# W_out to W_up in a hybrid encoder layer: combinations of normalised tokens moved to GpSimd, and two groups of transposes swapped

## The chip, the core and the metric

The kernel runs on one core of a Trainium2 chip. The metric is device time in microseconds (us) of one execution; lower is better. The core has five engines with instruction queues of their own: TensorE (PE: matrix products, and the transposes of this kernel), VectorE (DVE), ScalarE (ACT), GpSimd (POOL) and SyncE (SP, which here issues DMA transfers). Each queue runs in order, and engines wait for each other by semaphores. TensorE writes to PSUM, of which this kernel has eight banks of 128 x 512 numbers: two each of the kinds mm, s, t and o.

## What is computed

The reference runs one encoder layer over two groups of tokens (a "sample" of 512 and a "prompt" of 1024), with shared weights. This case lies in the prompt, between the output projection and the MLP:

```python
x = x + mixed @ w_out
a = jax.nn.relu(rmsnorm(x, g_mlp) @ w_up)
return x + (a * a) @ w_down
```

`rmsnorm` divides each token by the root of the mean of its squares and multiplies by a gain. The products have float32 accuracy. The kernel reaches it by splitting every operand into a rounded part (hi) and the rest (lo) and adding three products per pair of operands.

## The kernel before

**Place and tiles.** `Halves.project_out` handles the prompt's 1024 tokens in 8 tiles of 128. It takes 16 steps, one for each tile and each half (0 or 1) of the 1024 output channels, in the order that `steps` lists. Step n runs `product(n, t, half)`: 24 matmuls into a bank of kind mm or o (line 128), then VectorE adds the bank to the tile (L1250). The last step is n = 15.

**Normalising.** When a tile has both halves, `norm` (L173 to L183) normalises it: ScalarE squares and sums it (L173), then VectorE takes three one-column steps with one input (L174, L176, L178), six one-column steps with two inputs (L181 and L182, three times each, called the small steps) and one pass over the tile (L183). The eight normalised tiles come in four pairs, i = 0 to 3; k counts the tiles, so a pair is complete at odd k.

**Combinations.** The product with W_up is a fast (Strassen-like) scheme over quarters of the operands. For its seven products it needs quarters of the tokens (b11, b21, b22) and combinations of them (t1, t2, t3, t4). Of each pair the kernel forms four combinations of 128 x 512, tiles h0, h1 or y1, by four subtractions (L1285), all on VectorE:

```python
for to, x, y in ((h1[0], k1, o1), (h2[0], k2, h1[0]), (h2[1], k2, k1), (h1[1], o2, h2[0])):
    nc.vector.tensor_tensor(out=to, in0=x, in1=y, op=ALU.subtract)
```

**Turns.** `turn` transposes one piece of 128 x 512 (L1212): four transposes into a bank of kind t or s, in turn; then two casts on ScalarE (L132) write the hi parts and two subtractions on VectorE (L133, the evictions) the lo parts. The bank is free when all four are done. Which turns follow which product stands in `due`: after step n `flush(n)` runs the list `due[n]`. Pairs 0 and 1 are turned after steps 12 and earlier. After step 15 stand five turns of pair 2 (b22, t1, t2, t3, t4) and behind them two of pair 3 (b11, b21).

**The end of the step.** Then the first group of W_up begins inside `project_out`: the product b11 (12 matmuls into a bank mm), a copy of that bank by ScalarE (L1316, tile r_hi), the product b21 into the same bank, and `flush(16)`, the last five turns, of pair 3. After them `up` goes on with the other products of the scheme; I call that the up phase.

**Weight work beside it.** `ahead` prepares W_up's first group step by step from n = 7 on: ScalarE casts hi parts (L1338), POOL subtracts lo parts and forms weight combinations (L1335; tiles w_raw, x, y). Before the change POOL has nothing else to do here.

**What sets the order.** The program is written as above, and a scheduler of the build then orders each engine's queue by its own estimate of when an instruction can run, within the written dependences; `pinned` and `behind` hold some instructions to a place. So an edit at one place can move instructions of other lines on the same engine.

Of the kernel before, what the change touches and what calls it, by code (L numbers as in the profile page):

```python
# [22 lines left out]
ALU = mybir.AluOpType  # L23
# [1137 lines left out]
class Halves:  # L1161
# [55 lines left out]
    def project_out(self, hp, mp, m, wo):  # L1217

        layer, nc, nt, TH = self.layer, self.nc, self.nt, self.TH
# [8 lines left out]
        due = {}  # L1228

        def flush(n):  # L1230
            with layer.behind(layer.mark((mybir.EngineType.PE,))):
                for x in due.pop(n, ()):
                    self.turn(*x)
# [3 lines left out]
        def product(n, t, half):  # L1237
            ts = slice(t * 128, (t + 1) * 128)
            cs = slice(half * 512, (half + 1) * 512)
            w = wo[4 * half:4 * half + 4]  # L1240
            ops = [(m[kt // 2][0][:, kt % 2, ts], m[kt // 2][1][:, kt % 2, ts], w[kt // 2][0][:, kt % 2], w[kt // 2][1][:, kt % 2])
                   for kt in range(8)]
            if n < 2 and n not in banks:

                banks[n] = layer.psum(("mm", "o")[n % 2])
                layer.mm3(banks[n], ops[:6])
                return
            ps = banks[n] if n < 2 else layer.psum(("mm", "o")[n % 2])
            layer.mm3(ps, ops[6 if n < 2 else 0:], more=n < 2)
            nc.vector.tensor_tensor(out=acc[t][:, cs], in0=acc[t][:, cs], in1=ps, op=ALU.add)  # L1250
# [3 lines left out]
        steps = [(t, 0) for t in order[:nt // 2]]  # L1254
# [8 lines left out]
        for n, (t, half) in enumerate(steps):  # L1263
            product(n, t, half)
            if n == freed:
                b["t2"], b["t3"] = ([layer.pair(hp, [128, 2, TH], "hid", 4) for _ in range(2)] for _ in range(2))
                for x in due.pop("free"):
                    due[n].append(x[:1] + (b[x[1]],) + x[2:])
            flush(n)
            if half:  # L1270
                k = len(hn)
                nc.sync.dma_start(self.sums[t], acc[t])

                hn.append(acc[order[k - 1]] if k else self.tile("y0"))
                layer.norm(acc[t], gain, hn[k])
                i = k // 2
                at = n + (2 if n < len(steps) - 2 else 1)
                k1, k2 = hn[k][:, :512], hn[k][:, 512:]
                if k % 2 == 0:
                    due.setdefault(at, []).extend([(k1, b["b11"], i), (k2, b["b21"], i)])  # L1280
                else:
                    o1, o2 = hn[k - 1][:, :512], hn[k - 1][:, 512:]
                    h1, h2 = ((x[:, :TH], x[:, TH:]) for x in (self.tile("h1"), self.tile("y1" if i == 1 else "h0")))
                    for to, x, y in ((h1[0], k1, o1), (h2[0], k2, h1[0]), (h2[1], k2, k1), (h1[1], o2, h2[0])):
                        nc.vector.tensor_tensor(out=to, in0=x, in1=y, op=ALU.subtract)  # L1285
                    due.setdefault(at, []).append((k2, b["b22"], i))
                    due[at].append((h1[0], b["t1"], i))
                    for src, q in ((h2[0], "t2"), (h2[1], "t3")):
                        if q in b:
                            due[at].append((src, b[q], i))  # L1290
                        else:
                            due.setdefault("free", []).append((src, q, i))
                    due[at].append((h1[1], b["t4"], i))
            if n >= len(steps) // 2 - 1:
                with layer.pinned():
                    next(ahead, None)
# [2 lines left out]
        self.fetch(2)  # L1299
        self.begun = begun = [self.begin(mp)]  # L1300
        self.product(begun[0][0], self.w[0], 0, "b11")
        with layer.pinned():
            next(ahead, None)
        self.second(*begun[0], self.w[0])
# [382 lines left out]
```

## Time and profile before

| | us |
|---|---|
| three timed runs | 2009.88, 2016.78, 2017.57 |
| their median | 2016.78 |
| the profiled execution | 2014.83 |
| its span in the trace | 2013.0 |
| the edited stretch in it (last output product to the up phase) | 1364.5 to 1389.4 |

All times below are counted from the start of the profiled execution's span. Its mean granted TensorE clock is 0.989 of full speed. In a timeline row the first two numbers are start and duration; a row with "x4" stands for four instructions of one kind. In names, `out<-in` gives the tiles written and read. "idle before" is how long the engine stood still, and the name behind the arrow is what released it.

### The profile page before, as it was taken

To read this page: it belongs to the slowest core of one execution; us is meant where nothing else is said; L and a number is where in the kernel's file an instruction comes from. 1 tells how busy PE (TensorE), PEld (TensorE's weight loads), DVE (VectorE), ACT (ScalarE), POOL (GpSimd) and SP (SyncE) were. 2 spreads that over 40 slices of the span, in tenths; PEclk is the share of its full clock that TensorE was granted. 3 is DMA by queue.
4 is the path that set the end of the run, shared out by engine and by line. 5 is a ranking of instruction groups with operands and counts; after the bars stand their busy time and mean duration, and the time that the engine had idled before them with its cause. 6 is when DMAs were issued, how large, how long until landed. Compare 5 with 4: busy or idle time off the path is not lost.

```text
span 2013.0 us, 26474 instructions
## 1 busy us (share of the span) xinstructions
PE 1954.8 (97%) x9635; PEld 1625.1 (81%) x9635; DVE 1098.2 (55%) x1916; ACT 757.7 (38%) x1325; POOL 958.6 (48%) x743
## 2 busy tenths in 40 slices
PE   6999999999999999999999999999999999999997
PEld 4887787888888878888888888887888888888886
DVE  6572445756666552566663225466666666443246
ACT  3564323433332331556552313224333333433342
POOL 3144535467776740223333223413978774644442
PEclk8999999999999999999999999999999999999999
DMA  6666773354444445455555543412444445976663
GB/s 203 170 161 200 217 228 94 96 178 157 147 156 158 150 154 200 114 139 137 135 180 174 136 118 98 160 63 85 177 168 168 172 154 193 299 236 205 194 193 122
DMA packets 275652, 326.50 MB, mean 162 GB/s; under 512 B 42872, under 2 KB 197240, under 8 KB 274968
## 3 DMA queue, kind: packets, MB, share of 16 engines
q1 hardware_dynamic: 261792, 303.92, 47.6%
q0 software_dynamic: 13728, 20.88, 4.5%
q8 instruction: 76, 1.25, 0.3%
q14 instruction: 56, 0.46, 0.1%
HBM read 235.67 MB, written 91.64 MB: 163 GB/s over the span
## 4 chain that ended last, share of the span: by engine, by line
PE 83%; DVE 6%; DMA 4%; issue 2%; ACT 2%; POOL 2%; SPq 0%; POOLq 0%; DVEq 0%; ACTq 0%
PE ps_mm L128 23%; PE ps_o L128 22%; PE ps_s L128 19%; PE ps_t L128 8%; PE ps_mm L487 2%; PE ps_mm L488 2%; PE ps_mm L489 2%; PE ps_o L629 1%; DMA w_raw<-in_w_in 1%; POOL w_lo L152 1%; PE ps_t L609 1%; DMA bm<-g_un 1%; PE ps_t L193 1%; DMA gain<-in_w_fnB 1%; DVE st L182 1%
## 5 line engine op out<-in xcount | busy, mean ns | idle before, releaser
L152 POOL TENSOR_TENSOR w_lo<-w_raw,w_hi 128x1024 fp32r<-128x1024 f32 x84 | 212.7, 2540 | 210.2 <-ACT w_hi L151 180.3
L151 ACT CAST w_hi<-w_raw 128x1024 fp32r<-128x1024 f32 x100 | 104.7, 1048 | 156.4 <-PE ps_s L128 49.9
L487 PE MATMUL ps_mm<-hT,w_hi 128*128 128x512 f32 (+3 forms) x320 | 126.5, 395 | 0.2 <-DVE k L527 0.2
L1088 DVE TENSOR_TENSOR relu<-relu 128x512 f32<-128x512 f32 (+1 forms) x35 | 63.0, 1801 | 108.0 <-ACT relu L1087 108.0
L488 PE MATMUL ps_mm<-hT,w_hi 128*128 128x512 f32 (+3 forms) x320 | 115.2, 360 | 0.0
L489 PE MATMUL ps_mm<-hT,w_lo 128*128 128x512 f32 (+3 forms) x320 | 115.2, 360 | 0.0
L603 ACT ACTIVATE sc<-sc,ast 128x288 f32<-128x288 f32 (+4 forms) x96 | 53.9, 561 | 76.5 <-DVE ast L601 76.2
L1335 POOL TENSOR_TENSOR x<-w_hi,x 128x512 fp32r<-128x512 f32 (+1 forms) x42 | 69.8, 1662 | 23.0 <-ACT x L1338 23.0
L723 POOL MEMSET bm<- 64x96 f32 (+2 forms) x64 | 11.2, 175 | 144.7 <-DVE ast L601 97.7
L152 POOL TENSOR_TENSOR w_lo<-r,w_hi 128x1024 fp32r<-128x1024 f32 x15 | 36.8, 2452 | 87.5 <-ACT w_hi L151 87.5
L629 PEld LDWEIGHTS ps_o<-pt,vb 104*64 104x64 f32 (+6 forms) x576 | 62.3, 164 | 12.2 <-POOL vb L566 4.7
L152 POOL TENSOR_TENSOR w_lo<-w_hi 128x1024 fp32r<-128x1024 f32 x18 | 45.9, 2550 | 50.0 <-ACT w_hi L151 45.8
L152 POOL TENSOR_TENSOR w_lo<-w_lo,w_hi 128x1024 fp32r<-128x1024 f32 x18 | 48.0, 2668 | 45.2 <-ACT w_hi L151 45.2
L489 PEld LDWEIGHTS ps_mm<-hT,w_lo 128*128 128x128 f32 x320 | 60.4, 189 | 8.6
L629 PE MATMUL ps_o<-pt,vb 104*64 104x128 f32 (+6 forms) x576 | 63.4, 245 | 4.0 <-POOL vb L566 2.1
L566 POOL TENSOR_TENSOR vb<-vr,vb 96x384 fp32r<-96x384 f32 (+4 forms) x48 | 48.7, 1032 | 35.6 <-ACT vb L565 30.5
L128 PE MATMUL ps_t<-gate,x 128*128 128x512 f32 x264 | 65.3, 396 | 0.0
L128 PE MATMUL ps_mm<-gate,x 128*128 128x512 f32 x256 | 64.3, 395 | 0.0
L487 PEld LDWEIGHTS ps_mm<-hT,w_hi 128*128 128x128 f32 x320 | 60.9, 190 | 2.2 <-PE ps_s L597 0.4
L488 PEld LDWEIGHTS ps_mm<-hT,w_hi 128*128 128x128 f32 x320 | 61.0, 191 | 1.7
L601 DVE CUSTOM_DVE_ANT_0 sc<-ps_s,bm 128x288 f32<-128x288 f32 (+4 forms) x96 | 46.3, 482 | 24.4 <-PE ps_s L597 13.7
L152 POOL TENSOR_TENSOR w_lo<-raw,w_hi 128x512 fp32r<-128x512 f32 x24 | 35.5, 1485 | 50.5 <-ACT w_hi L151 42.2
(664 smaller groups left out, 5872.4 us busy)
## 6 DMA issues: line engine op xcount, KB each, us to landing
w_raw<-in_w_in SPq DMA_DIRECT2D x56, 512.0 KB
w_raw<-in_w_up SPq DMA_DIRECT2D x34, 512.0 KB
wt<-hn SPq DMA_DIRECT2D x32, 512.0 KB
hidden_prompt<-h SPq DMA_DIRECT2D x32, 512.0 KB
w_hi<-hidden_prompt SPq DMA_DIRECT2D x20, 512.0 KB
w_raw<-hidden_prompt SPq DMA_DIRECT2D x18, 512.0 KB
w_lo<-hidden_prompt SPq DMA_DIRECT2D x18, 512.0 KB
w_raw<-in_w_out SPq DMA_DIRECT2D x16, 512.0 KB
```

Of the source, the lines that this page charges most:

```text
L128: self.nc.tensor.matmul(out, a, b, start=(i == 0 and not more), stop=(i == len(terms) - 1), skip_group_check=more)
L151: nc.scalar.copy(out=hi, in_=raw)
L152: (lo_engine or nc.gpsimd).tensor_tensor(out=lo, in0=raw, in1=hi.bitcast(F32), op=ALU.subtract)
L487: nc.tensor.matmul(ps, a[0], b[0], start=(kt == 0), stop=False)
L488: nc.tensor.matmul(ps, a[0], b[1], start=False, stop=False)
L489: nc.tensor.matmul(ps, a[1], b[0], start=False, stop=(kt == 7))
L566: nc.gpsimd.tensor_tensor(out=lo, in0=vs, in1=hi.bitcast(F32), op=ALU.subtract)
L601: nc.vector.tensor_tensor_reduce(out=sc[:, :W], in0=ps[:, :W], in1=bm[:, :W], scale=1.0, scalar=3e38, op0=ALU.add, op1=ALU.min, accum_out= ...
L603: nc.scalar.activation(out=sc[:, :W], in_=sc[:, :W], func=AF.Exp, bias=st[:, 0:1], scale=-1.0, accum_out=st[:, 1:2])
L629: nc.tensor.matmul(po[:m, j * 128:(j + 1) * 128], v, x, start=(i == 0), stop=(i == len(ops) - 1))
L1088: nc.vector.tensor_tensor(out=r, in0=r, in1=r, op=ALU.mult)
L1335: self.nc.gpsimd.tensor_tensor(out=to, in0=x, in1=y, op=op)
```

## The change

It does two things, both in `project_out`. Of the pairs 0, 1 and 2 all four combinations go from VectorE to POOL, and of pair 3 one (the fourth of the new order) does. And after step 15 the two turns of pair 3 for b11 and b21 come first, then b22 and t1 of pair 2; the other three turns of pair 2 (t2, t3, t4) wait until the product b11 has been issued.

```diff
...
+            if n == len(steps) - 1:
+
+                x = due[n]
+                due[n], due["first"] = x[-2:] + x[:2], x[2:-2]
             flush(n)
...
-                    for to, x, y in ((h1[0], k1, o1), (h2[0], k2, h1[0]), (h2[1], k2, k1), (h1[1], o2, h2[0])):
-                        nc.vector.tensor_tensor(out=to, in0=x, in1=y, op=ALU.subtract)
+
+                    for j, (to, x, y) in enumerate(((h1[0], k1, o1), (h2[0], k2, h1[0]), (h1[1], o2, h2[0]), (h2[1], k2, k1))):
+                        (nc.gpsimd if i < nt // 2 - 1 or j == 3 else nc.vector).tensor_tensor(out=to, in0=x, in1=y, op=ALU.subtract)
...
         self.product(begun[0][0], self.w[0], 0, "b11")
+        flush("first")
```

In the rows of the order below, x_12122 is the second normalised tile of pair 2 and x_12126 the first of pair 3; h_12746 and h_12747 hold pair 2's combinations. On TensorE behind step 15, before the change (ps_mm with gate is b11, then b21):

```order
L1212 MATMUL ps_s<-ident,x_12122 128x128 x4
L1212 MATMUL ps_t<-ident,h_12746 128x128 x4
L1212 MATMUL ps_s<-ident,h_12747 128x128 x4
L1212 MATMUL ps_t<-ident,h_12747 128x128 x4
L1212 MATMUL ps_s<-ident,h_12746 128x128 x4
L1212 MATMUL ps_t<-ident,x_12126 128x128 x4
L1212 MATMUL ps_s<-ident,x_12126 128x128 x4
L128 MATMUL ps_mm<-gate,y_12495 128x512 x8
L128 MATMUL ps_mm<-gate,x_12496 128x512 x4
L128 MATMUL ps_mm<-gate,y_12495 128x512 x8
L128 MATMUL ps_mm<-gate,x_12496 128x512 x4
```

Here all seven turns stand ahead of the first product. On TensorE at the same place, with the change:

```order
L1212 MATMUL ps_s<-ident,x_12126 128x128 x4
L1212 MATMUL ps_t<-ident,x_12126 128x128 x4
L1212 MATMUL ps_s<-ident,x_12122 128x128 x4
L1212 MATMUL ps_t<-ident,h_12746 128x128 x4
L128 MATMUL ps_mm<-gate,y_12495 128x512 x8
L128 MATMUL ps_mm<-gate,x_12496 128x512 x4
L1212 MATMUL ps_s<-ident,h_12747 128x128 x4
L1212 MATMUL ps_t<-ident,h_12747 128x128 x4
L1212 MATMUL ps_s<-ident,h_12746 128x128 x4
L128 MATMUL ps_mm<-gate,y_12495 128x512 x8
L128 MATMUL ps_mm<-gate,x_12496 128x512 x4
```

The two turns of x_12126 have moved from the end of the list to its head, and three turns from before the product to behind its twelve matmuls.

On POOL from pair 1's end to pair 3, before the change, only weight work (L1335) stands there:

```order
L1335 TENSOR_TENSOR x_12562<-w_raw,x_12562 128x512
L1335 TENSOR_TENSOR w_raw<-w_raw 128x512 x2
L1335 TENSOR_TENSOR y_12563<-w_raw,y_12563 128x512
L1335 TENSOR_TENSOR x_12564<-w_raw,x_12564 128x512
L1335 TENSOR_TENSOR x_12565<-w_raw,x_12565 128x512
L1335 TENSOR_TENSOR x_12566<-w_raw,x_12566 128x512
```

The weight combinations (w_raw) follow each other directly. On POOL with the change (L1290 are the combinations, L1341 the weight work; x_12123 is the second normalised tile of pair 3):

```order
L1290 TENSOR_TENSOR h_12746<-x_12122,x_12125 128x512
L1290 TENSOR_TENSOR h_12747<-x_12122 128x512
L1290 TENSOR_TENSOR h_12747<-x_12122,h_12746 128x512
L1341 TENSOR_TENSOR w_raw<-w_raw 128x512
L1290 TENSOR_TENSOR h_12746<-x_12125,h_12747 128x512
L1341 TENSOR_TENSOR w_raw<-w_raw 128x512
L1341 TENSOR_TENSOR y_12563<-w_raw,y_12563 128x512
L1290 TENSOR_TENSOR h_12889<-x_12123 128x512
L1341 TENSOR_TENSOR x_12564<-w_raw,x_12564 128x512
L1341 TENSOR_TENSOR x_12565<-w_raw,x_12565 128x512
L1341 TENSOR_TENSOR x_12566<-w_raw,x_12566 128x512
```

The weight combinations (w_raw) now stand among the token combinations, and the last combination, of pair 3, stands ahead of the lo parts x_12564 to x_12566.

On VectorE around the second tile of pair 3, before the change (x_12123 is written by L183, then come its combinations; ps_s and ps_t are evictions):

```order
L178 TENSOR_SCALAR st<-st 128x1
L181 SCALAR_TENSOR_TENSOR st<-st 128x1
L182 SCALAR_TENSOR_TENSOR st<-st 128x1
L181 SCALAR_TENSOR_TENSOR st<-st 128x1
L182 SCALAR_TENSOR_TENSOR st<-st 128x1
L181 SCALAR_TENSOR_TENSOR st<-st 128x1
L182 SCALAR_TENSOR_TENSOR st<-st 128x1
L183 SCALAR_TENSOR_TENSOR x_12123<-x_12127,st,gain 128x1024
L1285 TENSOR_TENSOR h_12915<-x_12123,x_12126 128x512
L1285 TENSOR_TENSOR h_12916<-x_12123 128x512
L1285 TENSOR_TENSOR h_12916<-x_12123,h_12915 128x512
L1285 TENSOR_TENSOR h_12915<-x_12126,h_12916 128x512
```

Nothing stands between the six small steps. On VectorE with the change (h_12888 and h_12889 are pair 3's combinations):

```order
L133 TENSOR_TENSOR hid_lo<-ps_s,hid_hi 128x2x128
L182 SCALAR_TENSOR_TENSOR st<-st 128x1
L133 TENSOR_TENSOR hid_lo<-ps_t,hid_hi 128x2x128
L181 SCALAR_TENSOR_TENSOR st<-st 128x1
L133 TENSOR_TENSOR hid_lo<-ps_s,hid_hi 128x2x128
L182 SCALAR_TENSOR_TENSOR st<-st 128x1
L133 TENSOR_TENSOR hid_lo<-ps_t,hid_hi 128x2x128
L183 SCALAR_TENSOR_TENSOR x_12123<-x_12127,st,gain 128x1024
L133 TENSOR_TENSOR w_lo<-ps_s,w_hi 128x2x128
L1290 TENSOR_TENSOR h_12888<-x_12123,x_12126 128x512
L1290 TENSOR_TENSOR h_12889<-x_12123,h_12888 128x512
```

The small steps were in one piece and now stand between the evictions of pair 2's last three turns (hid_lo), and one combination has left.

## Rows read from the trace of the kernel before

**Rows 1.** The page, its part 1: busy us (share of the span) xinstructions of each engine.

```profile
PE 1954.8 (97%) x9635; PEld 1625.1 (81%) x9635; DVE 1098.2 (55%) x1916; ACT 757.7 (38%) x1325; POOL 958.6 (48%) x743
```

**Rows 2.** The waits of PE, 1290 to 1420 us: us in total, times, longest us.

```profile
PE ps_s L1212 <- DVE gate L133: 3.6, 1, 3.6
PE ps_mm L128 <- ACT r_hi L1316: 0.7, 1, 0.7
PE ps_t L1212 <- DVE gate L133: 0.6, 1, 0.6
```

**Rows 3.** The timeline of PE: start us, us, engine, line, operation, xcount [idle before <-releaser].

```profile
1350.24 0.60 PE L1212 MATMUL ps_t<-ident,h 128*128 128x128 f32 x4
...
1370.10 0.60 PE L1212 MATMUL ps_s<-ident,x 128*128 128x128 f32 x4
...
1371.40 0.60 PE L1212 MATMUL ps_t<-ident,h 128*128 128x128 f32 x4
1375.61 1.09 PE L1212 MATMUL ps_s<-ident,h 128*128 128x128 f32 x4 [3.60 <-DVE gate L133]
...
1378.05 3.57 PE L128 MATMUL ps_mm<-gate,y 128*128 128x512 f32 x8
...
1383.23 2.12 PE L128 MATMUL ps_mm<-gate,y 128*128 128x512 f32 x8 [0.68 <-ACT r_hi L1316]
...
1386.13 0.60 PE L1212 MATMUL ps_t<-ident,x 128*128 128x128 f32 x4
...
1389.36 0.43 PE L128 MATMUL ps_s<-hid_hi,y 128*128 128x512 f32 x1
```

**Rows 4.** Stretches: us, busy of PE, PEld, DVE, ACT, POOL, then PEclk, DMA share, GB/s.

```profile
1372.00:1378.00 6.00, 2.40 (x13) 2.42 (x12) 4.84 (x14) 3.87 (x10) 1.28 (x1) 0.70 0.87 245
1378.00:1383.20 5.20, 4.56 (x14) 3.22 (x12) 4.49 (x14) 1.82 (x5) 0.00 (x0) 0.69 0.00 0
1383.20:1389.00 5.80, 5.15 (x31) 4.37 (x32) 4.13 (x9) 2.56 (x8) 0.00 (x0) 1.00 0.00 0
1389.00:1412.00 23.00, 23.00 (x101) 18.38 (x100) 9.04 (x14) 9.28 (x16) 16.88 (x13) 1.00 0.21 65
```

**Rows 5.** By source, lines L1285 and L133: duration ns min/median/max, first and last start us, forms.

```profile
L1285 DVE TENSOR_TENSOR h<-x,h x5: 683/684/1603, 1320.9 to 1385.0; 128x512 f32<-128x512 f32 x5
...
L133 DVE TENSOR_TENSOR gate<-ps_s,gate x16: 410/424/426, 1314.6 to 1388.8; 128x256 fp32r<-128x256 f32 x16
```

**Rows 6.** The timeline of POOL, 1354 to 1369 us.

```profile
1354.55 2.67 POOL L1335 TENSOR_TENSOR w_raw<-w_raw 128x512 f32<-128x512 f32 x2
1367.13 1.29 POOL L1335 TENSOR_TENSOR y<-w_raw,y 128x512 fp32r<-128x512 f32 x1 [9.91 <-ACT y L1338]
```

**Rows 7.** The timeline of DVE, 1342 to 1383 us: normalised tiles (L183).

```profile
1342.40 1.28 DVE L183 SCALAR_TENSOR_TENSOR x<-x,st,gain 128x1024 f32<-128x1024 f32 x1
...
1363.43 1.28 DVE L183 SCALAR_TENSOR_TENSOR x<-x,st,gain 128x1024 f32<-128x1024 f32 x1
...
1372.23 1.28 DVE L183 SCALAR_TENSOR_TENSOR x<-x,st,gain 128x1024 f32<-128x1024 f32 x1
...
1381.71 1.28 DVE L183 SCALAR_TENSOR_TENSOR x<-x,st,gain 128x1024 f32<-128x1024 f32 x1
```

**Rows 8.** The timeline of ACT at 1366 us.

```profile
1366.36 0.18 ACT L173 ACTIVATION_READ_ACCUMULATOR x<-x 128x1 f32 x1
```

**Rows 9.** The timeline of all engines near the start, 11 to 17 us.

```profile
11.31 5.32 POOL L152 TENSOR_TENSOR w_lo<-w_raw,w_hi 128x1024 fp32r<-128x1024 f32 x2 [8.76 <-ACT w_hi L151]
...
12.16 0.15 DVE L178 TENSOR_SCALAR st<-st 128x1 int32<-128x1 int32 x1
...
12.35 1.95 DVE L181 SCALAR_TENSOR_TENSOR st<-st 128x1 f32<-128x1 f32 x1
...
14.33 2.32 DVE L182 SCALAR_TENSOR_TENSOR st<-st 128x1 f32<-128x1 f32 x1
...
16.69 0.22 DVE L181 SCALAR_TENSOR_TENSOR st<-st 128x1 f32<-128x1 f32 x1
```

## The prediction, made before the change was run

> **What bounds the kernel now.** I began with the page: TensorE is busy 97% of the span [rows 1]. A change that touches only VectorE, GpSimd and the order of some transposes can therefore give back no more than the time in which TensorE stands still or runs slowly near it. So the second view was the waits of TensorE around the edited step: there are only three between 1290 and 1420 us, 3.6, 0.7 and 0.6 us [rows 2]. The third view was TensorE's own timeline there [rows 3]. After the last output product (it ends where the first transpose starts, 1370.10) four turns run, then TensorE stands still for 3.60 us; three more turns follow, then b11 (from 1378.05), a 0.68 us wait, b21 (from 1383.23), five turns with a 0.62 us wait among them, and the first product of W_up proper at 1389.36. The reader should also see that the same instruction costs two prices: a turn takes 0.43 us before the stall (three from 1370.10 to 1371.40) and 0.81 behind it (three from 1375.61 to 1378.05). The table by stretches says why: the granted clock falls to 0.70 and 0.69 of full in the two stretches from 1372 to 1383, back to 1.00 behind them [rows 4]. That is the lower level, 1.2 GHz, taken in part of these stretches after TensorE had stood still. With all waits and the low clock taken out, the stretch from 1370.10 to 1389.36 would be 7.6 us shorter (3.6 + 0.7 + 0.6 of waits, 1.1 on three turns, 1.6 on b11, which took 4.5 where b21 took 2.9). That is 0.4% of the time, and the most that this change can win.
>
> **Pairs 0 and 1: no cost.** Moving the combinations takes four 0.68 us instructions [rows 5] off VectorE for each of these pairs. One on POOL takes 1.29 to 1.33 us [rows 6]. For pair 1 the second normalised tile is ready at 1343.68 [rows 7]. POOL now has four combinations and one weight combination in a row, so the last is done about 5 x 1.27 = 6.4 us later, at 1350.05; the turn that reads it starts at 1350.24 [rows 3]. The margin is 0.2 us, so I take 0, at worst 0.3. Pair 0 has over 1 us. The two weight combinations that now stand behind pair 1 feed ScalarE casts that come later anyway.
>
> **Pair 2: POOL becomes a row of seven.** Its second tile is ready at 1364.71 [rows 7]. From there POOL runs three combinations, a weight combination, the fourth combination, another weight combination and y_12563, back to back; these weight combinations were done at 1354.55 before [rows 6]. At 1.33 us each the ends are 1366.1, 1367.4, 1368.8, 1370.1, 1371.4, 1372.8 and 1374.1.
>
> In the same time VectorE must normalise the first tile of pair 3 (x_12126). Its sum of squares is read out at 1366.54 [rows 8]; behind the one-input steps and two evictions its six small steps (L181, L182) can start at 1367.6. Left alone they take 6 x 0.22 = 1.3 us [rows 9] and L183 1.28, so the tile would be ready at 1370.2, just when TensorE wants it.
>
> They are not left alone. At 11.31 POOL runs two subtractions [rows 9]. The first small step on VectorE takes 1.95 us, the next 2.32, each ending as a POOL instruction ends, and the one behind POOL's last takes 0.22. L178, with one input, takes its 0.15 beside POOL. So a VectorE instruction with two inputs in SBUF waits for the POOL instruction in flight, and between two of POOL's exactly one gets through. The longest combination of before, 1.60 against 0.68 us [rows 5], met POOL's instruction at 1367.13 [rows 6] in the same way. Applied here, five of the six small steps end with POOL's third to seventh instruction, the fifth at 1374.1; the sixth and L183 bring the tile to 1375.6. It was ready at 1373.51 before [rows 7]. The lock costs between 0 and 5.4 us; I take 5.4, since the small steps are the same instructions as in the rows.
>
> The Trainium skill (SBUF — State Buffer, Who interferes with whom) gives this as a rule: a VectorE instruction with two SBUF inputs contends with a GpSimd instruction that reads SBUF, and whichever issues first holds the shared port for the whole instruction. [...]
>
> **TensorE's new order.** The turns of x_12126 now come first, so TensorE stands still from 1370.1 to 1375.7: 5.6 us in place of 3.6. It had fallen to 1.2 GHz after a shorter stand, so I take the low clock for what follows. Four turns at 0.81 end at 1379.0. A matmul of b11 costs 0.43 us at the low clock (twice its price at the full one, where b21's twelve take 2.9 with a short start); I use 0.43 and 0.24; the clock came back near 1381.3, as the mean of 0.69 over the 1378 to 1383.2 stretch says [rows 4]. That ends b11 at 1382.9, against 1382.5 before: +0.4. The three turns behind b11 cover the copy of r_hi, so the 0.68 wait goes, but they take 1.3 themselves. b21 starts at 1384.2 and ends at 1387.1 against 1386.13: +1.0 so far.
>
> **The tail, pair 3.** In the new VectorE order the small steps of the second tile (x_12123) stand between the evictions of the three turns behind b11. They can't finish before those turns have run and been evicted: the copy of r_hi, which stands ahead on ScalarE, 0.68 [rows 2]; a cast 0.4; four evictions of 0.42 [rows 5] that overlap a little, 1.5; small steps that don't fit between, 0.45; L183 1.28. So the tile is ready 4.3 us after b11, at 1387.2 (call it T; before it was 1382.99, over 3 us ahead of its use [rows 3, 7]). TensorE is there at 1387.1, so the last five turns have lost their cover. POOL takes its one combination, T+0.1 to T+1.4, and holds the first one of VectorE until T+2.0. POOL's next (x_12564) then waits in turn, runs to T+3.2 and holds VectorE's second until T+3.8; the third ends at T+4.75. The last turn also needs a bank that four more evictions free at T+6.1. So the up phase starts at T+6.5 = 1393.7 against 1389.36. **Sum: +4.3 us**, made of +0.4 to the end of b11, +0.6 to the end of b21, +0.1 of waiting for x_12123 and +3.2 in the last five turns. What comes behind is bound by TensorE (23.00 of 23.00 us busy in the next stretch [rows 4]) and the other engines' casts move with it, so the shift carries to the end. The profiled execution took 2014.8 us, which gives 2019.1. The median of the three runs lies 2.0 us above that execution, inside their own spread of 7.7 us; I keep the sum on the profiled one.
>
> **Rivals.**
> Designed effect, without the lock. If the small steps slip in between POOL's instructions, x_12126 is ready at 1370.2, the clock does not fall, four turns end at 1372.0, b11 with a short wait at 1375.2, three turns and b21 at 1379.4; x_12123 is ready 4.3 us after b11, at 1379.5. Unlocked, its three combinations on VectorE end at T+2.7, the bank is free at T+4.0, and the up phase starts at T+4.4 = 1383.9, 5.5 us earlier: 2009.3. For it speaks that POOL's weight work may stall and open gaps; against it [rows 9].
> Slower by more. The tail has TensorE busy for about 2.2 us of 6. If the clock falls there again, or does not come back from the first fall, the rest of b11, three turns, b21 and the first two products of W_up run at 1.2 GHz, where twelve matmuls cost 5.2 instead of 2.9 us: +1.3, +1.2, +2.3 and 2 x 2.3 on top of +4.3, so about +13.7 and 2028.5. It decides from the point where TensorE's waits in the tail add up to about the one stand that brought the clock down before. Against it: the waits of 0.7 and 0.6 us left the clock at 1.00 behind 1383 [rows 2, 4].
> Nothing at all. If the idle time only changes its name (from the bank to x_12126) and the tail keeps its cover, the result is 2014.8; that lies in the forecast's own range. That the change is not carried out is excluded by the order of the built program.
>
> **How the numbers follow.** Forecast 0.65, its own range 2015 to 2023: the low end if the clock stays up in the first stand (four turns and b11 then end at 1380.5, -2.4) and POOL's second instruction in the tail comes late (-1.2), the high end if a second low stretch costs as much as the first (1.1 + 1.6), and a bound of 1 us on the times that I read off by hand. Designed effect 0.22, slower by more 0.08, anything unseen 0.05. Half a per cent is 10 us, about what a measurement of this kernel can tell from no change; neither the forecast nor the designed effect reaches it. Faster by more than that gets 0.04 (what spills over from the designed effect with the spread of the runs), slower 0.11 (the second rival and a spill of the forecast), the rest 0.85. The range for 8 in 10 takes in the designed effect, with the same bound of 1 us below it, and the forecast up to a second fall of the clock: 2008 to 2027.
>
> **What would show it.** In the profile of the changed kernel: TensorE waiting once, for x_12126, from about 1370 to 1375; small steps L181 and L182 of over 1 us beside POOL there; a stretch at half clock behind it; no wait for r_hi; waits of 1 to 2 us between the last five turns, and combinations on VectorE of over 1 us. The prediction is wrong if x_12126 is ready before 1372, or if the last five turns run without waits.

## The result, and the profile after

| | before | after |
|---|---|---|
| median of 20 runs each | 2013.48 us | 2018.71 us |
| ratio after / before, 95% interval | | 1.0026 (1.0020 to 1.0033) |
| the profiled execution | 2014.83 us | 2020.32 us |
| its span, its mean granted clock | 2013.0 us, 0.989 | 2018.6 us, 0.987 |

The change makes the kernel slower by 5.2 us in the medians and by 5.5 us between the two profiled executions. That is about a quarter of a per cent, as forecast (2019.1). The page shows what it did in sum: VectorE has 6 us less work than in [rows 1], POOL 12 us more, and TensorE 3 us more, though it runs the same 9635 matmuls.

```profile
PE 1957.7 (97%) x9635; PEld 1626.9 (81%) x9635; DVE 1092.0 (54%) x1903; ACT 757.2 (38%) x1325; POOL 970.3 (48%) x756
```

TensorE's waits between 1290 and 1430 us answer to [rows 2]. The wait for a free bank (3.6) has become a wait for a normalised tile (4.8), the wait for r_hi is gone, and two waits for combinations and a short one for a cast are new:

```profile
PE ps_s L1212 <- DVE x L183: 4.8, 1, 4.8
PE ps_s L1212 <- DVE h L1290: 1.4, 1, 1.4
PE ps_t L1212 <- DVE h L1290: 1.0, 1, 1.0
PE ps_o L128 <- ACT hid_hi L132: 0.5, 1, 0.5
```

Its timeline, to be read beside [rows 3] (start us, us, then the instruction and the idle time before it):

```profile
1369.13 1.07 PE L128 MATMUL ps_o<-r_hi,gate 128*128 128x512 f32 x4
1374.96 1.09 PE L1212 MATMUL ps_s<-ident,x 128*128 128x128 f32 x4 [4.76 <-DVE x L183]
...
1378.26 3.16 PE L128 MATMUL ps_mm<-gate,y 128*128 128x512 f32 x8
...
1382.18 0.60 PE L1212 MATMUL ps_s<-ident,h 128*128 128x128 f32 x4
...
1385.35 1.10 PE L128 MATMUL ps_mm<-gate,x 128*128 128x512 f32 x4
1386.44 0.63 PE L1212 MATMUL ps_t<-ident,x 128*128 128x128 f32 x4
1388.43 0.63 PE L1212 MATMUL ps_s<-ident,h 128*128 128x128 f32 x4 [1.36 <-DVE h L1290]
1390.10 0.63 PE L1212 MATMUL ps_t<-ident,h 128*128 128x128 f32 x4 [1.05 <-DVE h L1290]
...
1393.42 0.78 PE L128 MATMUL ps_s<-hid_hi,y 128*128 128x512 f32 x1
```

Up to the end of b21 almost nothing is lost. Counted from the start of the last four matmuls of the 16th output product (1369.18 before, 1369.13 after), b11 ends 0.2 us earlier than before and b21 0.2 us later. The last five turns then take 7.1 us (1386.3 to 1393.42) where they took 3.2 before. The last row shows something else: its matmul takes 0.78 us, and 0.43 in [rows 3]. The stretches show why (us, busy of PE, PEld, DVE, ACT, POOL, then PEclk):

```profile
1375.00:1378.20 3.20, 3.20 (x16) 3.20 (x17) 1.47 (x6) 2.12 (x6) 0.00 (x0) 0.50 0.58 179
1378.20:1382.20 4.00, 4.00 (x15) 3.16 (x15) 2.77 (x11) 1.83 (x6) 0.00 (x0) 0.71 0.41 123
1382.20:1386.40 4.20, 4.20 (x25) 3.36 (x23) 3.08 (x9) 2.16 (x6) 0.00 (x0) 1.00 0.00 0
1386.40:1393.40 7.00, 4.10 (x22) 2.79 (x22) 6.75 (x12) 3.08 (x9) 2.94 (x2) 0.81 0.00 1
1393.40:1398.40 5.00, 5.00 (x15) 4.00 (x14) 1.31 (x4) 3.00 (x6) 2.77 (x3) 0.58 0.00 0
```

The clock falls to 1.2 GHz twice: behind the first stand, as before [rows 4], and again behind the waits of the tail, where before it stayed at 1.00. The first product of the up phase therefore takes 4.8 us (1393.42 to 1398.2) in place of 2.8. From 1398.4 to 1420 TensorE is busy for 21.60 of 21.60 us at 1.00, as in [rows 4]: the shift is carried on.

The cause stands on VectorE and POOL. First beside the first tile of pair 3 (x_12126): POOL's row of seven, its first and last instruction, and VectorE's small steps in the same time:

```profile
1364.55 1.30 POOL L1290 TENSOR_TENSOR h<-x,x 128x512 f32<-128x512 f32 x1 [10.19 <-DVE x L183]
...
1372.02 1.26 POOL L1341 TENSOR_TENSOR y<-w_raw,y 128x512 fp32r<-128x512 f32 x1
```

```profile
1367.20 0.14 DVE L178 TENSOR_SCALAR st<-st 128x1 int32<-128x1 int32 x1
1367.38 0.99 DVE L181 SCALAR_TENSOR_TENSOR st<-st 128x1 f32<-128x1 f32 x1
1368.40 1.22 DVE L182 SCALAR_TENSOR_TENSOR st<-st 128x1 f32<-128x1 f32 x1
...
1372.12 1.18 DVE L181 SCALAR_TENSOR_TENSOR st<-st 128x1 f32<-128x1 f32 x1
1373.33 0.16 DVE L182 SCALAR_TENSOR_TENSOR st<-st 128x1 f32<-128x1 f32 x1
1373.53 1.28 DVE L183 SCALAR_TENSOR_TENSOR x<-x,st,gain 128x1024 f32<-128x1024 f32 x1
```

Five small steps of one column take 0.99 to 1.22 us each, four of them as long as a POOL instruction of 512 columns, and each ends with one; the sixth, when POOL is done (1373.28), takes 0.16. The same shows in the tail, beside the second tile (x_12123, ready at 1386.30): VectorE's first two combinations take 1.73 and 1.64 us in place of 0.68, and POOL's x_12564 takes 1.71 in place of 1.28.

```profile
1385.02 1.28 DVE L183 SCALAR_TENSOR_TENSOR x<-x,st,gain 128x1024 f32<-128x1024 f32 x1
...
1386.55 1.73 DVE L1290 TENSOR_TENSOR h<-x,x 128x512 f32<-128x512 f32 x1
1388.32 1.64 DVE L1290 TENSOR_TENSOR h<-x,h 128x512 f32<-128x512 f32 x1
```

```profile
1386.47 1.27 POOL L1290 TENSOR_TENSOR h<-x 128x512 f32<-128x512 f32 x1 [13.19 <-PE ps_mm L128]
1387.70 1.71 POOL L1341 TENSOR_TENSOR x<-w_raw,x 128x512 fp32r<-128x512 f32 x1
```

### The profile page after: what moved, and what is told of

It reads as the page before. It is cut to its first block, busy times and chain, and to the rows that moved or that the text cites. A ratio compares the mean times of both kernels' runs of the same rounds, so it can differ in the third digit from the quotient of the medians.

```text
span 2018.6 us, 26476 instructions
## 1 busy us (share of the span) xinstructions
PE 1957.7 (97%) x9635; PEld 1626.9 (81%) x9635; DVE 1092.0 (54%) x1903; ACT 757.2 (38%) x1325; POOL 970.3 (48%) x756
## 3 DMA queue, kind: packets, MB, share of 16 engines
q8 instruction: 76, 1.25, 0.3%
## 4 chain that ended last, share of the span: by engine, by line
PE 84%; DVE 6%; DMA 4%; issue 2%; POOL 2%; ACT 2%; SPq 0%; POOLq 0%; DVEq 0%; ACTq 0%
PE ps_mm L128 23%; PE ps_o L128 22%; PE ps_s L128 19%; PE ps_t L128 8%; PE ps_mm L487 3%; PE ps_mm L488 2%; PE ps_mm L489 2%; PE ps_o L629 2%; PE ps_t L609 1%; POOL w_lo L152 1%; DVE st L182 1%; DMA gain<-in_w_fnB 1%; DVE st L181 1%; PE ps_t L193 1%; PE ps_s L596 0%
## 5 line engine op out<-in xcount | busy, mean ns | idle before, releaser
L1341 POOL TENSOR_TENSOR x<-w_hi,x 128x512 fp32r<-128x512 f32 (+1 forms) x42 | 66.6, 1587 | 25.6 <-ACT x L1344 25.6
```

What stands on the lines that cost most here:

```text
L1341: self.nc.gpsimd.tensor_tensor(out=to, in0=x, in1=y, op=op)
```

## The experiments

Twelve kernels were run. Four theories stand against each other in what was expected. A: VectorE's steps with two SBUF inputs wait for POOL's instructions, and the low clock follows TensorE's longer stands (the prediction's own). B: the new order of turns costs it. C: the stand for pair 3's first tile is the whole loss. D, after the first four runs: the place of the second tile's norm in VectorE's queue costs the tail.

The differences are a tenth of a per cent, so beside the ratio of the times (of the kernel and of before, on the same chip) the table gives a second measure from each profiled execution: **the stretch**, from the start of the last four matmuls of the 16th output product to VectorE's read of the third bank of the up phase (1369.18 to 1397.76 before). It leaves out the run-to-run spread of the rest of the kernel. It has a spread of its own: the kernel with pairs 0 and 1 only does before's work in this stretch in before's order and is 0.7 us shorter, since the clock came back sooner in b11 (its first eight matmuls took 2.90 us, 3.57 in [rows 3]). Differences under 1 us of it mean nothing. It is taken from one execution of each kernel, and for pair 2 and pair 3 on VectorE it points another way than the ratio (shorter than before by 0.9 with a ratio of 1.0008, longer by 1.0 with 0.9999). "Tile 1" is when x_12126 is ready, from the stretch's start; "tile 2" when x_12123 is, from the end of b11, 0.93 us behind the start of its last four matmuls (in before the bank, and not tile 1, ended the stand). Before was run again with each group of kernels, with medians from 2012.07 to 2013.48 us, so ratios and not medians are to be compared between rows. Two further kernels, halves and zeros, were looked at in the trace only.

| kernel | median us | ratio (95%) | stretch us | tile 1 | tile 2 |
|---|---|---|---|---|---|
| before | 2013.48 | 1 | 28.6 | 4.3 | 0.6 |
| after | 2018.71 | 1.0026 (1.0020, 1.0033) | 34.6 | 5.7 | 4.1 |
| order alone | 2011.66 | 0.9989 (0.9979, 0.9999) | 27.5 | 4.3 | 1.2 |
| POOL alone | 2015.50 | 1.0013 (1.0004, 1.0021) | 31.0 | 5.7 | 1.1 |
| pair 2 on VectorE | 2013.61 | 1.0008 (0.9998, 1.0018) | 27.7 | 4.3 | 0.9 |
| pair 3 on VectorE | 2012.39 | 0.9999 (0.9989, 1.0009) | 29.6 | 5.7 | 4.1 |
| norm first | 2017.35 | 1.0025 (1.0016, 1.0034) | 32.1 | 5.7 | 2.2 |
| weights first | 2014.79 | 1.0012 (1.0003, 1.0021) | 30.0 | 3.8 | 4.1 |
| pairs 0 and 1 only | 2012.33 | 1.0001 (0.9992, 1.0010) | 27.8 | 4.3 | 1.3 |
| mended | 2010.56 | 0.9994 (0.9983, 1.0004) | 26.8 | 3.2 | 1.8 |
| mended 2 | 2011.02 | 0.9992 (0.9982, 1.0002) | 27.0 | 2.1 | 2.6 |
| mended, all on VectorE | 2011.85 | 1.0000 (0.9991, 1.0009) | 26.8 | 2.8 | 2.6 |

### One part of the change at a time

**Order alone**: the change without its edit of the combinations; all of them stay on VectorE, in the old sequence.

```diff
-                    for j, (to, x, y) in enumerate(...):
-                        (nc.gpsimd if i < nt // 2 - 1 or j == 3 else nc.vector).tensor_tensor(...)
+                    for to, x, y in ((h1[0], k1, o1), (h2[0], k2, h1[0]), (h2[1], k2, k1), (h1[1], o2, h2[0])):
+                        nc.vector.tensor_tensor(out=to, in0=x, in1=y, op=ALU.subtract)
```

> The new order of turns alone; every combination stays on VectorE. Theory A (the loss is VectorE's two-input steps standing behind POOL's instructions, and the low clock behind the longer stand of TensorE): without the row of seven on POOL the first tile of pair 3 is ready when it was before, about 1373.5; TensorE stands once, about 3.4 us; b11 ends about 1381.3; the second tile of pair 3 is ready 4.3 us behind that, its combinations take 0.68 each, and the up phase starts about 1390, +0.5 on before. Ratio to before 1.000, between 0.999 and 1.001. Theory B (the new order costs it, because the three turns of pair 2 and the second tile's norm lose their cover behind b11): the whole loss is here, ratio 1.0026.

Measured: 0.9989, so the order alone costs nothing; it may gain some 2 us, but the interval ends just under 1 (0.9999) and ten kernels were compared. Theory B falls. Theory A had the loss right but not the tail: it put tile 2 at 4.3 us behind b11, and it came at 1.2. TensorE's two waits in this stretch:

```profile
PE ps_s L1212 <- DVE x L183: 3.4, 1, 3.4
PE ps_t L1212 <- DVE hid_lo L133: 1.3, 1, 1.3
```

**POOL alone**: the kernel before with the change's edit of the combinations, in the old order of turns (the other half of the diff above).

> The combinations on POOL alone, in the old order of turns. Theory A: the first tile of pair 3 is ready at 1374.8 as with the whole change, and VectorE's evictions of pair 2 stand behind it, so that the fifth turn runs about 1.3 us later than before. The second tile of pair 3 still has b21 as cover, so the blocked combinations of the tail cost some 0.5 to 1.5 us: sum +1.3 to +2.8, ratio 1.0006 to 1.0014. Theory B (the order costs it): ratio 1.000, for POOL only relieves VectorE. Theory C (the lock is the whole loss, whatever the order): 1.0026.

Measured: 1.0013, as Theory A had it; B and C have their numbers outside the interval. The stand grows to 5.6 us, since pair 2's evictions stand behind tile 1's norm (the fifth turn runs 2.0 us later than before, 1.3 were expected), and the tail keeps b21 as its cover:

```profile
PE ps_s L1212 <- DVE gate L133: 5.6, 1, 5.6
PE ps_t L1212 <- DVE gate L133: 1.5, 2, 1.0
```

So one part gives -0.0011, the other +0.0013, and both together +0.0026: some 5 us of the loss are in neither part alone (each of the three numbers has an interval of about 0.001 to either side).

**Pair 2 on VectorE**, and **pair 3 on VectorE**: the whole change, with one pair's combinations put back.

```diff
-  (nc.gpsimd if i < nt // 2 - 1 or j == 3 else nc.vector)...
+  (nc.gpsimd if i < nt // 2 - 2 or (i == nt // 2 - 1 and j == 3) else nc.vector)...
```

That is pair 2 on VectorE, and this is pair 3:

```diff
-  (nc.gpsimd if i < nt // 2 - 1 or j == 3 else nc.vector)...
+  (nc.gpsimd if i < nt // 2 - 1 else nc.vector)...
```

> The whole change, but pair 2's four combinations back on VectorE; pairs 0 and 1 on POOL, and one of pair 3. Theory A: no small step of the first tile of pair 3 is blocked; it is ready at about 1373.5, the stand is 1.3 us shorter. The tail keeps its lock: the up phase starts 6.5 to 7.1 us behind the second tile, at 1392 to 1393, with or without a second low clock: ratio 1.0013 to 1.0025. Theory C (the stand behind the row of seven is the whole loss): 1.000. Theory B (order): 1.0026.

> The whole change, but pair 3's one combination back on VectorE. Theory A: the first stand stays as it is with the whole change (4.8 us, for the first tile of pair 3), and the second tile comes at 1386.3 as there; one POOL instruction of the weight work may still hold one combination of VectorE by 1.3 us. The up phase starts at 1390.7 to 1392.2 in place of 1393.4, and if the second fall of the clock hangs on the waits of the tail, it goes too: ratio 1.0006 to 1.0016. Theory C (the first stand is the whole loss): 1.0026 still.

Measured: 1.0008 and 0.9999. Both lie below Theory A's ranges, and Theory C (the stand for tile 1 is the whole loss) falls with the second: its stand is 4.80 us, like the whole change's, and the time is that of before. Each of the two takes away most of the loss or all of it, from different ends. With pair 2 back on VectorE, tile 2 is ready 0.9 us behind b11 and not 4.1. Two combinations are blocked here too, but by 0.8 us each, and they run beside b21 (1383.41 to 1386.3):

```profile
1383.69 1.45 DVE L1290 TENSOR_TENSOR h<-x,x 128x512 f32<-128x512 f32 x1
...
1385.40 1.44 DVE L1290 TENSOR_TENSOR h<-x,h 128x512 f32<-128x512 f32 x1
```

With pair 3 back, tile 2 is as late as with the change (4.1 us behind b11), but nothing blocks its combinations (0.68 us each): the waits of the tail are short, and the clock stays at 1.00 from 1383 on. Of its waits there:

```profile
PE ps_t L1212 <- DVE h L1290: 0.6, 1, 0.6
...
PE ps_s L1212 <- DVE h L1290: 0.3, 1, 0.3
```

That is what is in neither part alone: a late tile 2 and blocked combinations behind it. From the end of b21 to the up phase it is 3.2 us before and 4.9 with the order alone, 4.3 with blocked combinations behind an early tile 2 (pair 2 on VectorE), 5.0 with a late tile 2 and free combinations (pair 3 on VectorE), and 7.1 with both. The low clock is in the 7.1: halves (below), which has both too and no second low clock, takes 6.5. What makes tile 2 late is the new order of turns with POOL's row ahead of it: order alone has it at 1.2 us, POOL alone at 1.1, the kernels with both, where nothing else holds VectorE's queue, at 4.1. There the build's scheduler puts the norm's last small steps behind an eviction that can't run before b11 is done.

**Pairs 0 and 1 only**: the kernel before, with only these two pairs on POOL.

```diff
+  (nc.gpsimd if i < nt // 2 - 2 else nc.vector)...
```

> The kernel before, with the combinations of pairs 0 and 1 alone on POOL; pairs 2 and 3 and the order of turns as before. The prediction costed this at nothing (pair 1's last combination ends 0.1 to 0.2 us ahead of its turn, pair 0's over 1 us). If that holds: ratio 1.000 (0.9993 to 1.0007), no wait of TensorE before 1365 us that was not there before. Rival (a part of the loss comes from these pairs): 1.001 or more, with a wait of TensorE for one of their combinations near 1350 us.

Measured: 1.0001, and TensorE has no wait between 1290 and 1365 us, in this kernel as in before and after. These two pairs cost nothing.

### The lock by itself

**Halves**: the whole change, with pair 2's combinations on POOL written as two of 256 columns.

```diff
+  for c in (slice(0, 256), slice(256, 512)) if i == 2 else (slice(0, 512),):
+      (...).tensor_tensor(out=to[:, c], in0=x[:, c], in1=y[:, c], op=ALU.subtract)
```

> The whole change, with each of pair 2's four combinations on POOL written as two of 128x256; the weight combinations then stand behind all eight. Read from the trace only. Theory A (a two-input step of VectorE ends with the POOL instruction in flight, and one gets in between two): the small steps beside the halves take about 0.7 us each in place of 1.2, those beside the whole weight combinations 1.2 to 1.3; the first tile of pair 3 is ready between 1373.7 and 1375.2. Rival (POOL slows VectorE's steps to a fixed rate, whatever the size of its instruction): 1.2 us for each step.

Measured, the timeline of POOL and then of VectorE (L1291 are the combinations here, L1342 the weight work):

```profile
1366.71 2.84 POOL L1291 TENSOR_TENSOR h<-x,h 128x256 f32<-128x256 f32 x4
...
1370.90 2.61 POOL L1342 TENSOR_TENSOR w_raw<-w_raw 128x512 f32<-128x512 f32 x2
1373.47 2.25 POOL L1342 TENSOR_TENSOR y<-w_raw,y 128x512 fp32r<-128x512 f32 x1
```

```profile
1368.14 0.73 DVE L181 SCALAR_TENSOR_TENSOR st<-st 128x1 f32<-128x1 f32 x1
1368.90 0.67 DVE L182 SCALAR_TENSOR_TENSOR st<-st 128x1 f32<-128x1 f32 x1
...
1371.00 1.18 DVE L181 SCALAR_TENSOR_TENSOR st<-st 128x1 f32<-128x1 f32 x1
...
1372.41 2.18 DVE L183 SCALAR_TENSOR_TENSOR x<-x,st,gain 128x1024 f32<-128x1024 f32 x1
```

A half takes 2.84 / 4 = 0.71 us and the small steps beside halves 0.66 to 0.73; beside a whole weight combination 1.18. The step lasts until the POOL instruction that it meets ends, whatever its own size. L183 has two SBUF inputs as well. It starts beside the second weight combination, which ends at 1373.51, and takes 2.18 us in place of 1.28; y_12563, which starts at 1373.47, then waits for L183 and takes 2.25 in place of 1.26. So the waiting goes both ways.

This kernel shows one more thing, in the tail. TensorE's waits there are those of the change (1.3, 1.1 and 0.5 us, and 0.3 more), but the clock, the 1.00 in the row, does not fall behind them (us, busy of PE, PEld, DVE, ACT, POOL, PEclk):

```profile
1389.00:1394.00 5.00, 4.21 (x24) 3.24 (x23) 4.17 (x11) 3.55 (x11) 0.36 (x1) 1.00 0.00 0
```

**Zeros**: POOL writes zeros in place of three of pair 2's combinations, which are left out.

```diff
+  if i == 2 and j:
+      with layer.behind(layer.mark((mybir.EngineType.Pool,))):
+          for _ in range(4):
+              nc.gpsimd.memset(to, 0.0)
...
```

> The whole change, with three of pair 2's four combinations left out: POOL writes zeros to their tiles, each four times, so that it is busy with instructions that write SBUF and read none for as long as the small steps of pair 3's first tile run. Read from the trace only. If it is POOL's reads that hold VectorE's two-input steps: the small steps beside the writes of zeros take 0.16 to 0.22 us, those beside the weight combinations 1.2. If any POOL instruction holds them: each ends with the end of a write.

Measured (POOL, then VectorE):

```profile
1370.37 6.72 POOL L1293 MEMSET h<- 128x512 f32 x12
1377.06 2.62 POOL L1346 TENSOR_TENSOR w_raw<-w_raw 128x512 f32<-128x512 f32 x2
```

```profile
1371.96 0.22 DVE L181 SCALAR_TENSOR_TENSOR st<-st 128x1 f32<-128x1 f32 x1
...
1377.42 0.92 DVE L181 SCALAR_TENSOR_TENSOR st<-st 128x1 f32<-128x1 f32 x1
```

POOL is busy without a gap from 1370.37 to 1377.1, writing; all six small steps take 0.16 to 0.22 us. The first one that meets a weight combination, which reads, takes 0.92. So writes of POOL alone do not block; its instructions that read do. TensorE does not stand for tile 1 at all here. The Trainium skill (SBUF — State Buffer, Who interferes with whom) says this of reads and writes, and these rows agree.

**Weights first**: the whole change, with the two weight combinations ahead of pair 2's, where POOL is idle.

```diff
+            if n == 13:
+                with layer.pinned():
+                    next(ahead, None)
             if half:
...
-            if n >= len(steps) // 2 - 1:
+            if n >= len(steps) // 2 - 1 and n != 13:
```

> The whole change, with the two weight combinations on POOL ahead of pair 2's four combinations (where POOL is idle), so that its row from 1364.6 has four instructions and then y_12563 when ScalarE has cast it. Theory A (one small step for each POOL instruction in flight): two small steps end with POOL's third and fourth instruction at 1368.3 and 1369.6, four are free at 0.2, and the first tile of pair 3 is ready at 1371.7; if y_12563 meets the row, one more is blocked and it is 1373.0. TensorE stands 1.6 to 2.9 us in place of 4.8. The tail stays as it is. Ratio 1.0005 to 1.0018. Rival (the small steps are slowed by something else, such as the copies and DMA of the weights, not by POOL's instructions): still 1.2 us each, ready at 1374.8, ratio 1.0026.

Measured: 1.0012, inside Theory A's range, the rival's 1.0026 outside the interval. Three small steps are blocked, by POOL's third and fourth combination and by y_12563; the other three take 0.16 to 0.22 us:

```profile
1364.13 0.98 DVE L181 SCALAR_TENSOR_TENSOR st<-st 128x1 f32<-128x1 f32 x1
1365.15 0.16 DVE L182 SCALAR_TENSOR_TENSOR st<-st 128x1 f32<-128x1 f32 x1
1365.34 1.14 DVE L181 SCALAR_TENSOR_TENSOR st<-st 128x1 f32<-128x1 f32 x1
1366.52 1.19 DVE L182 SCALAR_TENSOR_TENSOR st<-st 128x1 f32<-128x1 f32 x1
```

Tile 1 comes 1.9 us earlier than with the change, the stand is 2.9 us, and b11 runs at the full clock. The tail is that of the change (waits of 1.4, 1.0 and 0.5 us, and a low clock behind them).

### The place of the second tile's norm

**Norm first**: the whole change, with the evictions of pair 2's last three turns held behind tile 2's norm and combinations.

```diff
-        flush("first")
+        with layer.behind(layer.mark((mybir.EngineType.DVE,))):
+            flush("first")
```

> The whole change, with the evictions of pair 2's last three turns held behind the norm and the combinations of pair 3's second tile on VectorE. POOL's row, and with it the first stand of 4.8 us, stays. Theory D (in the tail it is the place of that norm in VectorE's queue that costs: with the whole change two of its small steps stand behind an eviction that can't run before b11 is done, and the tile is ready at 1386.3; with the pairs' work in another mix it was ready at 1381.5 and 1383.1): the tile is ready about 1383.4, b21 covers it again, the up phase starts near 1390, and no second low clock: ratio 1.000 to 1.001. Theory A (the tail's loss is the two combinations behind POOL's, wherever the norm stands): the combinations are blocked as before, the evictions behind them come later, the up phase starts at 1392 to 1393: ratio 1.0015 to 1.0026.

Measured: 1.0025. Theory D's number is outside the interval: that tile 2 is ready 1.9 us sooner behind b11 doesn't pay. Two combinations are blocked as with the change, and now six evictions stand behind them; TensorE waits once, for a bank, and the clock falls behind that (0.72 in 1383 to 1389). Two combinations on VectorE, and the second of TensorE's last five turns:

```profile
1380.60 3.34 DVE L1290 TENSOR_TENSOR h<-x,h 128x512 f32<-128x512 f32 x2
...
1385.41 1.09 PE L1212 MATMUL ps_s<-ident,h 128*128 128x128 f32 x4 [3.19 <-DVE hid_lo L133]
```

### Versions meant to beat both

**Mended**: pair 2's first two combinations on POOL, its other two (behind tile 1's norm) and pair 3's on VectorE; the weight combinations and x_12564 ahead of pair 2's combinations on POOL; turns b22, b11, b21, t1; tile 2 ahead of the last evictions.

```diff
-                due[n], due["first"] = x[-2:] + x[:2], x[2:-2]
+                due[n], due["first"] = x[:1] + x[-2:] + x[1:2], x[2:-2]
...
+                    pooled = {0: (0, 1, 2, 3), 1: (0, 1, 2, 3), 2: (0, 1), 3: ()}[i]
+                        if i == 2 and j not in pooled:
+                            held.append((to, x, y))
...
+        with layer.behind(layer.mark((mybir.EngineType.DVE,))):
+            flush("first")
```

> A version after theories A and D: pairs 0 and 1 on POOL; of pair 2 the two combinations that come early on POOL and the other two on VectorE behind the norm of pair 3's first tile; all four of pair 3 on VectorE; POOL's weight work ahead of pair 2 (x_12564 before y_12563); the turn of b22 first, then b11 and b21, then t1; the norm of pair 3's second tile and its combinations ahead of the evictions of t2 to t4. Expected by A and D: the first tile of pair 3 ready at 1370.2 or before, TensorE's first stand under 1.5 us and no fall of the clock, up phase between 1383 and 1386.5: ratio 0.9965 to 0.9985. Rival (VectorE, which has some 15 us of work between 1370 and the up phase, is the bound whatever the order): no better than 1.000.

**Mended 2**: y_12563 one step later, and the two held combinations behind the evictions of the first four turns.

```diff
+            if n == 15:
+                with layer.behind(layer.mark((mybir.EngineType.DVE,))):
+                    for to, x, y in held:
+                        nc.vector.tensor_tensor(out=to, in0=x, in1=y, op=ALU.subtract)
...
-            if n >= len(steps) // 2 - 1 and n != 13:
+            if n >= len(steps) // 2 - 1 and n not in (13, 14):
```

> The mended version once more, with two edits: y_12563 on POOL one step later, so that it doesn't hold a small step of pair 3's first tile (it held one 1.29 us there), and pair 2's two late combinations on VectorE behind the evictions of the first four turns instead of ahead of them (1.2 us). Theory (what is left is these two): the first tile of pair 3 is ready 1.1 us earlier, b11 starts 2 us earlier, the stretch from the last output product's last four matmuls to the third product of the up phase, 28.6 us before and 26.8 in the first mended version, comes to 24.5 to 25.5: ratio 0.998 (0.9972 to 0.9988). Rival (VectorE's work behind 1370 is the bound): 26.8 again, ratio 0.9994.

**Mended, all on VectorE**: mended 2 with pair 2's first two combinations on VectorE too.

```diff
-                    pooled = {0: (0, 1, 2, 3), 1: (0, 1, 2, 3), 2: (0, 1), 3: ()}[i]
+                    pooled = {0: (0, 1, 2, 3), 1: (0, 1, 2, 3), 2: (), 3: ()}[i]
...
-                        if i == 2 and j not in pooled:
+                        if i == 2 and j > 1:
```

> The second mended version, but all four combinations of pair 2 on VectorE (two at once, two behind the evictions); POOL has the combinations of pairs 0 and 1 only. If POOL's two early combinations of pair 2 bring something, this one is slower than the second mended version by the 1.2 us that they take of VectorE, 0.0006. If VectorE has them in time that it idles anyway, the two are equal within 0.5 us.

Measured: 0.9994, 0.9992 and 1.0000. All three are faster than the change, none by the measurement faster than before, and my expectations of 0.9965 to 0.9988 were misses; the rivals' numbers came. No small step of tile 1 is blocked in the last two (TensorE waits 0.7 and 1.5 us for it, in place of 4.8), and still the stretch is as long as in the first mended version. What is left seems to be VectorE. The time from the last output product to the end of the last turn, in the kernel before and in the mended version that has all on VectorE:

```profile
1370.10:1389.40 19.30, 14.40 (x75) 11.99 (x74) 15.60 (x43) 9.69 (x27) 1.28 (x1) 0.82 0.39 105
```

```profile
1368.20:1385.30 17.10, 12.78 (x74) 9.63 (x72) 15.24 (x40) 8.95 (x26) 1.29 (x1) 1.00 0.50 139
```

VectorE is busy for 15.2 of 17.1 us here. What TensorE wins at its first stand it gives back to waits for VectorE's evictions (1.3 and 0.7 us in both late versions, and 0.8 for a cast of ScalarE). That VectorE is the bound is read from these numbers; no run shows it by itself. Whether POOL helps at all, which the last of the three asks, stays open: 0.9992 and 1.0000 have overlapping intervals, and the stretches are equal. But the equal stretches do not settle it: in mended 2 the clock fell in the tail (its last three turns start 0.85 us apart, 0.44 at the full clock, so some 1.2 us), and in the other version it did not.

## Why the prediction was right, point by point

**Pairs 0 and 1 at no cost**: right. Pair 1's last combination ended 0.12 us ahead of its turn, where 0.2 was forecast, and the kernel with these two pairs alone gives 1.0001.

**Pair 2's row on POOL**: the mechanism was right to the step: five of six small steps blocked, one for each POOL instruction. The term was slightly too big. I took 1.33 us for each of POOL's instructions, and back to back they take 1.25 (1364.55 to 1373.28 for seven). Tile 1 came at 1374.8, not 1375.6, and TensorE stood 4.8 us, not 5.6.

**The low clock and b11**: right, and too late by nearly the same 0.8 us: b11's end forecast 0.4 us later than before, measured 0.2 earlier. That is the tile's: four turns and b11 themselves took 7.2 us, as forecast. Four turns and b11 cost some 2.6 us more than at the full clock (3.3 for four turns that take 1.7, 3.9 for matmuls that take 2.9), as much as the low clock cost before.

**The tail**: right. Tile 2 came 4.1 us behind b11 (forecast 4.3), and the three combinations at T+2.0, T+3.7 and T+4.6 (forecast 2.0, 3.8 and 4.75). The up phase came at T+7.1 and not T+6.5: ScalarE's cast cost a wait of 0.46, and the last turns ran at the low clock.

**The step that was mis-sized** is the one that I kept as a bound only: a second fall of the clock. I argued against it from the waits of 0.7 and 0.6 us that had left the clock at 1.00 before. But the tail that I had forecast myself has waits of 1.4 and 1.0 us, and behind these the clock fell; it costs 2.0 us in the first product of the up phase. The sum was +4.3 us; the trace has 4.1 to the start of the up phase and 6.1 with this. The 4.1 is in part luck: +1.0 was forecast to the end of b21 and 0.2 measured, and the tail made up for it. Whether every execution of the changed kernel has the second fall is not shown: the profiled one (2020.32) is 1.6 us above the median, and with the same waits in halves the clock stayed up. That 2019.1 meets the median 2018.71 so closely owes something to the reference too: the profiled execution of before, on which I built, is 1.35 us above before's median of 20 runs, and between the medians the loss is 5.2 us.

**The rivals**: the designed effect (2009.3) needs tile 1 not to be blocked. Where that is so, with zeros or in the last two mended versions, TensorE's stand goes indeed, but 5.5 us do not come: I had left out that VectorE has 15 us of work in the same 17 us, which is the likeliest reason. "Slower by more" (2028.5) had its mechanism, a second low clock, but with one product at the low clock and not b11 and b21 as well. Its condition, waits that add up to about the first stand of before (3.6 us), does not decide by itself: the clock fell behind waits of 1.4 and 1.0 us here, and in halves not behind four that make 3.2.

## What to carry to other kernels

Before moving elementwise work from VectorE to GpSimd, look at what VectorE does in the same microseconds: each instruction of it with two inputs in SBUF, one column wide or a thousand, waits for a GpSimd instruction in flight that reads SBUF. A chain of tiny dependent steps suffers most, one whole GpSimd instruction for each step; so by these rows the place for the moved work is beside PSUM evictions, or where VectorE idles. And an edit of two parts is worth trying part by part: here one gains a little or nothing, the other loses a little, and together they lose twice as much; as the traces have it, each used up the other's cover.

## What was not expected of the hardware

- POOL had seven instructions in a row, and VectorE got one step in behind each, as forecast (0.99 us for the first of five, then 1.18 to 1.22). It need not be one: in weights first POOL's third combination ends at 1365.10 and its fourth starts at 1365.18, and the small step at 1365.15 slipped in at 0.16 us. The lock holds POOL too: 1.71 us for x_12564 beside VectorE's combinations, 2.25 beside L183, in place of 1.26 to 1.29.
- Evictions, with one input in PSUM, ran at 0.41 to 0.42 us beside POOL's reads, and L178, with one input, at 0.14.
- Writes of zeros on POOL (128x512) take 0.56 us each; the six small steps and L183 beside them take 0.16 to 0.22 and 1.28 us, as without POOL.
- Behind a stand of 2.85 us (weights first) the clock stayed at 1.00 for b11; behind 3.36 us (order alone) it read 0.69 in the stretch from 1373 to 1378. In the tails of the change and of weights first it fell behind waits of 1.4 and 1.0 us; in halves, with waits of 1.3 and 1.1, and in pair 3 on VectorE, with waits of 0.3 to 0.6, it did not. And with the same waits of 1.3 and 0.7 us in the tail it fell in mended 2 (0.80 in 1389 to 1394) and not in the version with all on VectorE. What decides was not tried.
